# Scan outputs one chunk later, row-half low-rank products, and three moved steps in a hybrid RWKV-7 / attention kernel

## The chip, the cores and the metric

One core of a Trainium2 chip runs the whole step in one launch. The metric is device time in microseconds (us), the median of several runs. The engines named below are PE (TensorE, matrix products), DVE (VectorE), ACT (ScalarE), POOL (GpSimd) and SP (the queue that issues DMAs). Each works through its own list in order.

## The reference, cut to what matters

Two layers work on 1024 latent and 256 context tokens of width 1024. Layer 0 is an RWKV-7 scan in both directions (8 heads of 64) beside a short convolution; layer 1 is grouped-query attention with 16 query and 4 key heads. Each layer is modulated by a vector made from a conditioning input:

```python
mod = silu(cond) @ w_ada + b_ada             # shift, scale, gate
h   = rmsnorm(x, g) * (1 + scale) + shift
# layer 0
w_log = -softplus(-(w0 + tanh(lw) @ lw2)) - 0.5      # low-rank products: 64 wide
decay = exp(-exp(w_log)); a = sigmoid(a0 + la @ la2)
# per head and token, forwards and backwards:
S = S * w_t - (S @ kk_t) (kk_t * a_t)^T + v_t k_t^T ;  y_t = S @ r_t
# layer 1: softmax(q k^T / 8 ...) v, gated, projected
```

## The kernel before, in words

All numbers are fp32. Where a big product is made, its operands are split into a high and a low part, and three matrix products take the place of one (`h_hi,whi`, `h_lo,whi`, `h_hi,wlo`). Every instruction is recorded through one helper, so nearly every row of the trace bears its line, L145; rows are told apart by the names of the tiles.

The order of the work is set while the program is built, by a planner (`Loom`). Each piece of work is a generator that says before each group of instructions what it needs (`yield "T", tiles, rings`: T is PE, V DVE, S ACT, G POOL, D a DMA); among the generators that are ready, the planner takes the first in a list of names (`PRECEDENCE`). The last ones in the list, the big products, fill the gaps. PSUM banks lie in small rings: `mm` (2 banks, the big products), `wk` (2), `py` (2), `iv` (1) and `ch` (1).

The stages, with their times in the trace:

- **0 to 64 us, setup.** Four tiles of x are loaded, then rows of small parameters (`prow`; among them `c` and `c_ctx`), transposed on PE, then eight tiles `wada` of the modulation's weights with three buffers (`ada`). 32 matmuls with `cond` give `mrow`, from which come `mod` and the first normalised inputs `h_hi`, `h_lo`.
- **64 to 1162 us, in-projection and scan.** 2448 big products `mm<-h_hi,whi` and so on run beside 20 scan steps. A step has two heads, two directions and four chunks of 64 tokens. `prepare` makes the low-rank products `iv<-lor,lw` and the decays; `interact` makes products of the keys of a chunk (`wk<-s,bk`) and transposes keys (`tbk`); `solve` inverts the 32 x 32 blocks by 62 DVE instructions on `acc`, which go through DRAM (`w_d`) to the tile `w`; `merge` joins the blocks of `w` to 64 x 64 ones, by `iv<-ident,w` (a transposition on PE), `iv<-t,nn` and `iv<-w,zz`; `chain` runs the four chunks.
- **1162 to 1575 us.** Out-projection of layer 0, then the products of layer 1: gate g0, keys and values, queries, gate g1 (`mm<-h_hi,wts`).
- **1575 to 2130 us, attention.** Maxima of the scores are taken first: pairs of products `kh,qh` (64 rows each), and a DVE reduction `mx` for each. After that come scores `qh,kh`, exponentials, and `pv<-pe,v_sb`.
- **2130 to 2252 us.** The last projection.

A chunk of `chain` has this sequence, each step in four small matmuls: `ch<-hv,s` (the state's part, `pa`); a copy of it to `xs`; `py<-s,hv` (the output's first part); `ch<-xs,w` (`pu`, with the inverse); copies of it to `hv`; `ch<-hv,tbk` (the next state's sum); four DVE instructions `hv<-ch,gc,hg` that make the next state; `py<-br,hv` (the output's second part); and taking both `py` banks out to `y`. The next chunk's `ch<-hv,s` needs the four new `hv`.

What starts a solve and an attention stage is held by two conditions:

```python
yield lambda: x.nr is not None and (x.n < 2 or steps[x.n - 2].done)   # all_solved
yield lambda: 1 not in wk_ps.busy.values()                            # all_moved, "attention"
```

Of the kernel before, what the change touches and what calls it, by code (L numbers as in the profile page):

```python
# [48 lines left out]
              ("evac", -0.1), ("h1", 1.0), ("x", -0.1), ("interacted", 0), ("solved1", 0), ("solved", 0),  # L49
# [67 lines left out]
class Loom:  # L117
# [128 lines left out]
    def issued(self, e, name, a, k, r):  # L246
# [9 lines left out]
        if e == "T":  # L256
# [3 lines left out]
            else:  # L260
                dur = max(0.054, n * (1 if ins[0].dtype == F32R else 4) / 2400.0)
                if ins[0].dtype == F32R and ins[0].partition_size() == 64:
# [66 lines left out]

    def run(self, gens):  # L330

        self.live = [[g, lambda: True, x] for g, x in gens]
# [35 lines left out]
def hybrid_step(  # L368
# [42 lines left out]
        ("c", c.rearrange("o (n p) -> (o n) p", p=P), 8),  # L411
        ("c_ctx", c_ctx.rearrange("(n p) -> n p", p=P), 8),
# [12 lines left out]
    with tc.tile_pool(name="prm", bufs=2, reuse_waits="tile") as prm:  # L425
        r0 = 0
        t0 = 0
# [39 lines left out]

    def ada(pool, cond, jobs):
# [72 lines left out]
    with tc.tile_pool(name="eyep", bufs=1, reuse_waits="tile") as eyep:  # L541
# [353 lines left out]
    def prepare(x):  # L895
# [11 lines left out]
        for d in range(2):  # L907
            yield "T", x.lor, lw2, iv_ps
            pz = iv_ps.take()
            for z in range(2):  # L910
                T.matmul(pz[:, z * GRP:(z + 1) * GRP], lw2[HH[d], z, :], x.lor[HH[d], z, :], start=True, stop=True)
            for z in range(2):
# [3 lines left out]
            iv_ps.release(pz)  # L916
# [64 lines left out]
    def interact(x):  # L981
# [40 lines left out]
        yield lambda: x.n < 2 or steps[x.n - 2].done  # L1022

        x.tbk = chn.tile([P, 2, 4, P], F32, tag="tbk", name="tbk")
# [16 lines left out]
    def solve(x):  # L1041
# [14 lines left out]
        x.solved = True  # L1056
        wdt = wd[x.n % 4]
        dma(out=wdt.rearrange("i p t -> p i t"), in_=acc)
        x.w = w_t[x.n % 2]
        w8 = x.w.rearrange(CD)  # L1060
        for hb_ in range(4):
            b = hb_ % 2
            dma(out=w8[hb_ * 32:hb_ * 32 + 32, :, b * 32:b * 32 + 32],
                in_=wdt.rearrange("i (q c r) t -> r (i q) c t", q=4, r=4)[hb_])

    def merge(x):
# [20 lines left out]
        yield "T", w8, iv_ps  # L1087
        pa = iv_ps.take()
# [6 lines left out]
        yield from copied(pa, *((t11[r:r + 32, :], pa[r:r + 32, 0:256]) for r in (0, 64)))  # L1095
        iv_ps.release(pa)
# [24 lines left out]
    def chain(x):  # L1121
# [33 lines left out]
        yield "T", x.hv[:, :, :, 0], x.s[0], x.s[1], x.w, ch_ps  # L1155
        pc = ch_ps.take()
        for i in range(4):
# [3 lines left out]
            for d in range(2):  # L1161
                for h, rr in enumerate(HH):
                    T.matmul(pa[rr, d], x.s[h][:, d, i, 0, :], x.hv[:, h, d, i, :], start=True, stop=True)
            xs = chn.tile([P, 2, C], F32, tag="xs", name="xs", bufs=1)
            yield from copied(pa, (xs, pa))
            yield "T", py_ps, py_ps
            pys = [py_ps.take(), py_ps.take()]
            for d in range(2):
                for h, rr in enumerate(HH):
                    T.matmul(pys[d][rr, 0:C], x.hv[:, h, d, i, :], x.s[h][:, d, i, 1, :], start=True, stop=False)  # L1170
# [29 lines left out]
            yield ("T",)  # L1200
            for d in range(2):
                for h, rr in enumerate(HH):
                    T.matmul(pys[d][rr, 0:C], x.hv[rr, h, d, i, :], x.br[rr, d, i, :], start=False, stop=True)
            for d in range(2):
                py = pys[d]
                yield "V" if j is not None and j >= 2 else "S", py, 0.15
                c0 = i * C if d == 0 else GRP - (i + 1) * C
                ysl = y[d][:, c0:c0 + C]
                if d == 1:
                    ysl = ysl[:, ::-1]  # L1210
                if (j is not None and j >= 2) or c0 in seen:
                    V.tensor_tensor(out=ysl, in0=py[:, 0:C], in1=ysl, op=ALU.add)
                else:
                    S.activation(ysl, py[:, 0:C], AF.Copy)
                if j is None:
                    seen.add(c0)
                py_ps.release(py)
            if i < 3:
                yield "T", x.hv[:, :, :, i + 1]
# [63 lines left out]
    V.memset(cond, 0.0)  # L1283
    S.activation(cond[:, :, 0], col("c", 0, 8), AF.Silu)
    S.activation(cond[:, :, 1], col("c_ctx", 0, 8), AF.Silu)
# [60 lines left out]
    with tc.high_priority():  # L1346
        for i in range(4):
            get_x(i)
# [1103 lines left out]
```

## Time and profile before

| what | us |
|---|---|
| median of 3 runs (lowest, highest) | 2257.18 (2255.88, 2263.26) |
| the profiled execution's own time | 2253.86 |
| its span, first to last instruction | 2252.2 |
| PE busy in it | 2052.1 (91%) |
| DVE busy | 1471.9 (65%) |
| ACT busy | 1052.1 (47%) |
| POOL busy | 1012.0 (45%) |
| mean granted clock of TensorE | 0.951 |

The span is what the trace covers; the execution's own time is 1.7 us longer. PE is the engine that is busy longest; whether it also sets the end in a stage is read from that stage's rows. A busy PE includes matrix products that wait in its pipeline, so intervals from one start to the next are better prices than durations.

### The profile page before, as it was taken

The numbers are of one execution on the slowest core, as the hardware profiler recorded it, in microseconds if no ns is written. First come the engines' busy times: TensorE is split into PE (matmuls) and PEld (weight loads), VectorE is DVE, ScalarE is ACT, GpSimd is POOL, SyncE is SP. The second block draws the span as 40 slices with busy tenths as digits, with TensorE's granted clock in tenths as the row PEclk, the third lists the DMA queues.
The fourth block names the chain that finished last, engine by engine and source line by source line (L and its number), as shares of the span: only waits on it lengthen the run. The fifth ranks groups of instructions, "written<-read, shape, count | busy, mean of one in ns | idle before, by whom it ended". The sixth has DMA issues, their size and how long they took to land.

```text
span 2252.2 us, 42921 instructions
## 1 busy us (share of the span) xinstructions
PE 2052.1 (91%) x15306; PEld 1411.7 (63%) x15306; DVE 1471.9 (65%) x3483; ACT 1052.1 (47%) x2476; POOL 1012.0 (45%) x1152
## 2 busy tenths in 40 slices
PE   4998889798988988998979999999999999999898
PEld 1486666576666666666657788888454545454487
DVE  2346878948888886868645733552877777775443
ACT  3446556645665556554435632221354444444422
POOL 2434344333344343333224321430487777888622
PEclk7999899999998999999889999999799999999899
DMA  7834344324433333342345633323321211102243
GB/s 271 305 98 131 98 105 131 85 68 114 102 97 103 99 96 101 85 111 54 86 153 185 206 111 88 99 87 107 82 53 48 60 42 38 43 28 71 58 131 108
DMA packets 337818, 232.86 MB, mean 103 GB/s; under 512 B 163890, under 2 KB 289860, under 8 KB 335556
## 3 DMA queue, kind: packets, MB, share of 16 engines
q1 hardware_dynamic: 337604, 230.12, 35.0%
q8 instruction: 120, 1.97, 0.4%
q14 instruction: 94, 0.77, 0.1%
HBM read 166.95 MB, written 57.75 MB: 100 GB/s over the span
## 4 chain that ended last, share of the span: by engine, by line
PE 39%; DVE 9%; DMA 5%; issue 3%; ACT 1%; POOL 1%; SPq 1%; DVEq 0%; POOLq 0%; ACTq 0%
PE mm L145 21%; PE pv L145 8%; PE wk L145 5%; PE py L145 4%; DVE mx L145 3%; DVE rz L145 1%; DVE zs L145 1%; DMA rz<-rz_d 1%; PE ch L145 1%; DVE tmp L145 1%; SPq L145 1%; DVE acc L145 1%; DMA rz_d<-rc 1%; DMA rc<-rz 0%; DVE hv L145 0%
## 5 line engine op out<-in xcount | busy, mean ns | idle before, releaser
L145 POOL TENSOR_TENSOR zs<-zs,pe 128x512 f32<-128x512 f32 x275 | 366.8, 1370 | 34.1 <-ACT pe L145 32.1
L145 PE MATMUL mm<-h_hi,whi 128*128 128x512 f32 (+1 forms) x816 | 336.5, 412 | 4.3 <-ACT whi L145 4.1
L145 PE MATMUL mm<-h_hi,wlo 128*128 128x512 f32 (+1 forms) x816 | 299.3, 367 | 8.1 <-DVE wlo L145 7.2
L145 PE MATMUL mm<-h_lo,whi 128*128 128x512 f32 (+1 forms) x816 | 298.7, 366 | 0.0
L145 POOL TENSOR_TENSOR wlo<-wraw,whi 128x128 fp32r<-128x128 f32 x228 | 111.4, 494 | 246.0 <-ACT whi L145 205.8
L145 PE MATMUL pv<-pe,v_sb 128*64 128x512 f32 (+1 forms) x832 | 200.4, 604 | 0.0
L145 PEld LDWEIGHTS mm<-h_hi,whi 128*128 128x128 f32 x816 | 159.9, 196 | 49.5 <-issue 12.2
L145 PEld LDWEIGHTS mm<-h_hi,wlo 128*128 128x128 f32 x816 | 160.1, 196 | 37.1 <-DVE wlo L145 10.0
L145 DVE TENSOR_TENSOR acc<-acc,tmp 128x60 f32<-128x60 f32 (+23 forms) x620 | 168.0, 273 | 20.8 <-issue 2.9
L145 PE MATMUL mm<-wts,omh 128*128 128x512 f32 x648 | 166.6, 410 | 7.6 <-ACT wts L145 4.0
L145 PEld LDWEIGHTS mm<-h_lo,whi 128*128 128x128 f32 x816 | 161.0, 197 | 14.4
L145 PE MATMUL mm<-wts,h_hi 128*128 128x512 f32 x480 | 151.1, 396 | 0.0
L145 POOL TENSOR_TENSOR hg<-hv,gc 64x128 f32<-64x128 f32 x152 | 65.1, 428 | 185.0 <-DVE hv L145 173.9
L145 PEld LDWEIGHTS mm<-wts,omh 128*128 128x128 f32 x648 | 122.9, 194 | 38.0 <-ACT wts L145 5.3
L145 ACT ACTIVATE whi<-wraw 128x128 fp32r<-128x128 f32 x272 | 80.2, 305 | 78.2 <-DMA wraw<-in_w_in_e_dram 40.3
L145 DVE TENSOR_REDUCE mx<-mm 128x1 f32<-128x512 f32 (+1 forms) x138 | 89.7, 660 | 36.7 <-PE py L145 12.6
L145 DVE SCALAR_TENSOR_TENSOR hv<-ch,gc,hg 64x64 f32<-64x64 f32 x288 | 81.3, 282 | 49.3 <-PE ch L145 42.2
L145 POOL TENSOR_TENSOR xr<-xr,og 128x512 f32<-128x512 f32 x40 | 54.6, 1364 | 128.4 <-DVE og L145 93.3
L145 PEld LDWEIGHTS pv<-pe,v_sb 128*64 128x64 f32 x832 | 51.6, 139 | 93.9 <-issue 82.3
L145 DVE TENSOR_REDUCE mx<-py 128x1 f32<-128x512 f32 (+1 forms) x138 | 89.6, 660 | 28.7 <-PE mm L145 13.0
L145 DVE TENSOR_TENSOR tmp<-acc,nra 128x31 f32<-128x31 f32 (+7 forms) x320 | 90.1, 282 | 27.4 <-DMA acc<-eye_d 17.7
L145 ACT ACTIVATE pe<-py 128x512 f32<-128x512 f32 (+1 forms) x139 | 79.1, 587 | 60.3 <-PE mm L145 20.3
(284 smaller groups left out, 5189.5 us busy)
## 6 DMA issues: line engine op xcount, KB each, us to landing
wraw<-in_w_in_e_dram SPq DMA_DIRECT2D x272, 64.0 KB
wada<-in_w_ada_dram SPq DMA_DIRECT2D x16, 1024.0 KB
inp<-rkv_d SPq DMA_DIRECT2D x40, 384.0 KB
om<-om_d SPq DMA_DIRECT2D x52, 256.0 KB
wraw<-in_w_in_o_dram SPq DMA_DIRECT2D x40, 256.0 KB
wada<-in_w_ada_dram SPq DMA_DIRECT2D x16, 512.0 KB
rkv_d<-nb SPq DMA_DIRECT2D x24, 256.0 KB
lor<-lora_d SPq DMA_DIRECT2D x40, 128.0 KB
```

What stands on the lines that cost most here:

```text
L145: r = f(*a, **k)
```

## The change

1. **Setup.** `c` and `c_ctx` get a tile of their own (`crow`), loaded first and transposed early, so that `cond` is there early. `wada` has five buffers, and five of its loads stand between the loads of x, ahead of the parameter rows.
2. **Low-rank products.** Both directions' banks are taken together (one of the ring `iv`, one of `wk`), and the four matmuls alternate between rows 0 to 63 and rows 64 to 127.
3. **`merge`.** The transposition of `w` on PE (16 matmuls and two copies a step) is made by two DVE transpositions.
4. **Conditions.** The transposition of keys (`tbk`) is a generator of its own. A solve no longer waits for the step two before it to be done; that wait stands now after the result's way to DRAM. Of two solves the older goes first.
5. **`chain`.** One `py` bank for a chunk. `py<-s,hv` stands right behind `ch<-hv,s`; `py<-br,hv` of a chunk right behind the next chunk's `ch<-xs,w`; `y` is taken out a chunk later.
6. **First maxima.** Those of the first three blocks use the two `py` banks, and attention's move of banks waits for them.
7. **Planner.** The cost that the planner books for 64-row matmuls now holds for fp32 too and only for over 64 columns; this changes the order alone.

```diff
@@ ada
-            wt = pool.tile([P, n * 512], F32, tag=f"wada{n}", name="wada")
+            wt = pool.tile([P, n * 512], F32, tag=f"wada{n}", name="wada", bufs=ADA if n == 4 else 3)
...
-        for _ in range(3):
-            get()
+        with tc.high_priority() if not loom.on else nullcontext():
+            for _ in range(3 if loom.on else ADA):
+                get()
+                if not loom.on and len(xts) < 4:
+                    get_x(len(xts))
@@ prepare
-        for d in range(2):
-            yield "T", x.lor, lw2, iv_ps
-            pz = iv_ps.take()
-            for z in range(2):
+        yield "T", x.lor, lw2, iv_ps, wk_ps
+        pzs = [iv_ps.take(), wk_ps.take()]
+        for z in range(2):
+            for d, pz in enumerate(pzs):
                 T.matmul(pz[:, z * GRP:(z + 1) * GRP], lw2[HH[d], z, :], x.lor[HH[d], z, :], start=True, stop=True)
@@ solve
-        x.solved = True
         wdt = wd[x.n % 4]
         dma(out=wdt.rearrange("i p t -> p i t"), in_=acc)
+        yield lambda: x.n < 2 or steps[x.n - 2].done
@@ merge
-        for i in range(8):
-            for h in range(2):
-                r1 = 64 * h
-                T.matmul(pa[r1:r1 + 32, i * 32:i * 32 + 32], w8[r1:r1 + 32, i, 0:32], ident[r1:r1 + 32, r1:r1 + 32],
-                         start=True, stop=True)
...
+        for rr in HH:
+            V.transpose(t11[rr].rearrange("p (i t) -> p i t", i=8), w8[rr, :, 0:32])
@@ chain
+        def by_u(i, py):
+
+            for d in range(2):
+                for h, rr in enumerate(HH):
+                    T.matmul(py[rr, d * C:d * C + C], x.hv[rr, h, d, i, :], x.br[rr, d, i, :], start=False,
+                             stop=(d == 1), skip_group_check=True)
...
+            if before:
+                by_u(i - 1, before)
             yield from copied(pu, *((x.hv[rr, h, :, i, :], pu[rr]) for h, rr in enumerate(HH)))
...
+            if before:
+                yield from put(i - 1, before)
+            before = py
@@ all_solved
-            yield lambda: x.nr is not None and (x.n < 2 or steps[x.n - 2].done)
+            yield lambda: x.ready
+            loom.yield_to(*("solved", "solved1") if b == 0 else ("solved1", "solved"))
@@ all_moved, all_first
-        yield lambda: 1 not in wk_ps.busy.values()
+        yield lambda: 1 not in wk_ps.busy.values() and "first" in moved
...
-            yield from maxima_of(k, 0, 1)
+            yield from maxima_of(k, 0, 1, py_ps)
+        yield lambda: not py_ps.busy
+        moved.add("first")
```

How the instructions stand now. The names are tiles as in the text above; a number behind a name tells one use of a bank or tile from another.

On PE, in the scan, one direction's low-rank products of a step (the other direction's stand some thirty rows away), before:

```order
L145 MATMUL mm_6939<-h_hi,whi 128x512
L145 MATMUL mm_6939<-h_lo,whi 128x512
L145 MATMUL mm_6939<-h_hi,wlo 128x512
L145 MATMUL iv_7202<-lor,lw_6969 128x256 x2
L145 MATMUL ch_6895<-hv,tbk 64x64 x4
```

and both directions' of a step, after:

```order
L145 MATMUL mm_7205<-h_hi,whi 128x512
L145 MATMUL mm_7205<-h_lo,whi 128x512
L145 MATMUL mm_7205<-h_hi,wlo 128x512
L145 MATMUL iv_7222<-lor,lw_7037 128x256
L145 MATMUL wk_7223<-lor,lw_7037 128x256
L145 MATMUL iv_7222<-lor,lw_7037 128x256
L145 MATMUL wk_7223<-lor,lw_7037 128x256
L145 MATMUL ch_6899<-hv,tbk 64x64 x4
```

The four matmuls of a step stand together, and neighbours write to different banks from different row halves.

On PE, in a chunk of the chain in the middle of the scan, from the next state's sum `ch<-hv,tbk` to the next chunk's `ch<-hv,s`, before:

```order
L145 MATMUL ch_12159<-hv,tbk 64x64 x4
L145 MATMUL iv_12318<-ident,vt 64x128 x4
L145 MATMUL py_12258<-br,hv 64x64 x2
L145 MATMUL py_12259<-br,hv 64x64 x2
L145 MATMUL mm_12269<-h_hi,whi 128x512
L145 MATMUL mm_12269<-h_lo,whi 128x512
L145 MATMUL mm_12269<-h_hi,wlo 128x512
L145 MATMUL ch_12159<-hv,s_10532 64x64
L145 MATMUL ch_12159<-hv,s_10533 64x64
L145 MATMUL ch_12159<-hv,s_10532 64x64
L145 MATMUL ch_12159<-hv,s_10533 64x64
```

and after, in a chunk from the product with the inverse on:

```order
L145 MATMUL ch_12255<-xs,w_198 64x64 x4
L145 MATMUL py_12260<-br,hv 64x64 x4
L145 MATMUL mm_12251<-h_hi,whi 128x512
L145 MATMUL mm_12251<-h_lo,whi 128x512
L145 MATMUL mm_12251<-h_hi,wlo 128x512
L145 MATMUL mm_12251<-h_hi,whi 128x512
L145 MATMUL mm_12251<-h_lo,whi 128x512
L145 MATMUL mm_12251<-h_hi,wlo 128x512
L145 MATMUL ch_12255<-hv,tbk 64x64 x4
L145 MATMUL mm_12251<-h_hi,whi 128x512
L145 MATMUL mm_12251<-h_lo,whi 128x512
L145 MATMUL mm_12251<-h_hi,wlo 128x512
```

`py<-br,hv` (now that of the chunk before) has left the stretch behind `ch<-hv,tbk` and stands beside `ch<-xs,w`; big products alone fill the stretch in which the DVE makes the next state.

On PE, at the end of gate g1's products, before, where no product `kh,qh` stands ahead of the last `mm<-h_hi,wts`:

```order
L145 MATMUL mm_17904<-h_hi,wts_17181 128x256
L145 MATMUL mm_17904<-h_hi,wts_17193 128x256
L145 MATMUL mm_17904<-h_lo,wts_17193 128x256
L145 MATMUL mm_17904<-h_hi,wts_17194 128x256
L145 MATMUL mm_17946<-kh_16675,qh_17576 128x512
L145 MATMUL mm_17948<-kh_16675,qh_17576 128x512
L145 MATMUL pv_17964<-kh_16675,qh_17576 128x512
L145 MATMUL py_17966<-kh_16675,qh_17576 128x512
```

and after:

```order
L145 MATMUL mm_17641<-h_lo,wts_16777 128x256
L145 MATMUL mm_17641<-h_hi,wts_16778 128x256
L145 MATMUL py_17689<-kh_16259,qh_17192 128x512
L145 MATMUL py_17691<-kh_16259,qh_17192 128x512
L145 MATMUL py_17696<-kh_16259,qh_17192 128x512
L145 MATMUL py_17698<-kh_16259,qh_17192 128x512
L145 MATMUL wk_17723<-ident,qt_17172 128x128 x4
L145 MATMUL pv_17731<-qh_17160,kh_16259 128x512
```

24 of the 26 pairs of the first maxima now stand among gate g1's products, about nine 512-column products apart; two pairs are left behind the last one, and the first scores `qh,kh` follow.

## Rows read from the trace of the kernel before

**Rows 1.** Busy time by stretch: us, PE, PEld, DVE, ACT, POOL, PEclk, DMA share, GB/s

```profile
14.00:20.00 6.00, 0.91 (x8) 0.25 (x12) 4.46 (x20) 1.11 (x3) 0.85 (x4) 1.00 1.00 418
100.00:1100.00 1000.00, 899.45 (x9092) 666.50 (x9092) 753.93 (x2155) 549.73 (x1439) 388.10 (x645) 0.95 0.37 100
1100.00:1160.00 60.00, 45.98 (x412) 28.40 (x410) 36.09 (x105) 23.21 (x57) 12.06 (x17) 0.77 0.44 136
1575.00:1585.00 10.00, 9.01 (x25) 4.12 (x25) 10.00 (x18) 1.63 (x3) 3.28 (x4) 0.84 0.97 275
1575.00:1604.50 29.50, 27.01 (x56) 12.79 (x56) 29.50 (x58) 4.15 (x7) 5.77 (x6) 0.62 0.60 154
```

**Rows 2.** Waits of PE, 100 to 1170 us: us in total, times, longest

```profile
PE ch L145 <- DVE hv L145: 19.7, 30, 2.8
PE ch L145 <- ACT hv L145: 7.0, 19, 1.5
```

**Rows 3.** Setup by time: start, us, engine, operation, [idle before <-releaser]

```profile
12.12 20.00 SPq L145 DMA_DIRECT2D wada<-in_w_ada_dram  x8
...
39.79 1.93 PE L145 MATMUL wk<-wada,cond 128*32 128x512 f32 x8 [2.61 <-DMA wada<-in_w_ada_dram]
41.79 0.69 DVE L145 COPY mrow<-wk 128x512 f32<-128x512 f32 x1 [23.10 <-PE wk L145]
```

**Rows 4.** PE groups of 0 to 1170 us: xcount, busy us, mean ns, idle before

```profile
L145 PE MATMUL iv<-lor,lw 64*128 64x256 f32 x160 | 48.8, 428 | 3.3 <-ACT bk L145 1.1 <-DMA lor<-lora_d 1.1 <-DVE y L145 0.7
L145 PE MATMUL iv<-ident,w 32*32 32x32 f32 x640 | 14.7, 195 | 4.5 <-DMA w<-w_d 1.9 <-DVE y L145 1.6 <-ACT sqy L145 0.6
```

**Rows 5.** PE by time in mid-scan

```profile
540.90 0.40 PE L145 MATMUL mm<-h_lo,whi 128*128 128x512 f32 x1
541.14 0.40 PE L145 MATMUL mm<-h_hi,wlo 128*128 128x512 f32 x1
...
558.81 1.13 PE L145 MATMUL iv<-lor,lw 64*128 64x256 f32 x4
559.87 0.45 PE L145 MATMUL ch<-hv,tbk 128*64 128x64 f32 x8
560.25 0.45 PE L145 MATMUL wk<-s,bk 64*64 64x128 f32 x8
560.52 0.34 PE L145 MATMUL py<-br,hv 64*64 64x64 f32 x6
...
562.14 0.45 PE L145 MATMUL wk<-s,bk 64*64 64x128 f32 x8
562.52 0.45 PE L145 MATMUL py<-s,hv 128*64 128x64 f32 x8
```

**Rows 6.** DVE groups of 0 to 1170 us

```profile
L145 DVE SCALAR_TENSOR_TENSOR hv<-ch,gc,hg 64x64 f32<-64x64 f32 x288 | 81.3, 282 | 49.3 <-PE ch L145 42.2 <-ACT bk L145 2.3 <-ACT nb L145 0.9
...
L145 DVE COPY hv<-iv 64x256 f32<-64x256 f32 x10 | 4.2, 418 | 0.2
```

**Rows 7.** PE by time, from gate g1's last product to attention

```profile
1573.98 0.28 PE L145 MATMUL mm<-h_hi,wts 128*128 128x256 f32 x1
...
1609.57 0.50 PE L145 MATMUL wk<-kh,qh 64*128 64x512 f32 x1
1609.91 0.39 PE L145 MATMUL mm<-qh,kh 64*128 64x512 f32 x1
...
1612.11 1.94 PE L145 MATMUL pv<-pe,v_sb 128*64 128x512 f32 x8
```

**Rows 8.** DVE by time, the same stretch

```profile
1563.73 0.69 DVE L145 SCALAR_TENSOR_TENSOR sgo<-sgo,mm 128x512 f32<-128x512 f32 x1 [4.91 <-ACT sgo L145]
...
1575.05 1.36 DVE L145 TENSOR_REDUCE mx<-mm 128x1 f32<-128x512 f32 x2
...
1590.51 0.20 DVE L145 STREAM_TRANSPOSE mt<-mx 128x32 f32<-128x32 f32 x1
```

**Rows 9.** The queue SP by time, the same stretch

```profile
1577.74 0.51 SPq L145 DMA_DIRECT2D v_sb<-v_d  x1
```

More of the change, by code (lines that the diff above doesn't have):

```diff
@@ L425, in hybrid_step @@
     with tc.tile_pool(name="prm", bufs=2, reuse_waits="tile") as prm:
+        with tc.high_priority():
+            crow = prm.tile([16, P], F32, name="crow", bufs=1)
+            for i, x in enumerate((c.rearrange("o (n p) -> (o n) p", p=P), c_ctx.rearrange("(n p) -> n p", p=P))):
+                dma(out=crow[8 * i:8 * i + 8, :], in_=x)
+            pt = py_ps()
+            T.transpose(out=pt[:, 0:16], in_=crow, identity=ident[0:16, 0:16])
+            V.tensor_copy(par[:, 0:16], pt[:, 0:16])
+        rows["c"], rows["c_ctx"] = 0, 8
         r0 = 0
-        t0 = 0
+        t0 = 16
         cur = prm.tile([P, P], F32, tag="prow", name="prow")
@@ L1153, in chain, with put @@
                 ch_ps.release(pt)
-        yield "T", x.hv[:, :, :, 0], x.s[0], x.s[1], x.w, ch_ps
+        def by_u(i, py):
[3 more added lines that the diff above has]
+                             stop=(d == 1), skip_group_check=True)
+        def put(i, py):
+            for d in range(2):
+                c0 = i * C if d == 0 else GRP - (i + 1) * C
+                ysl = y[d][:, c0:c0 + C]
+                if d == 1:
+                    ysl = ysl[:, ::-1]
+                add = (j is not None and j >= 2) or c0 in seen
+                yield "V" if add else "S", py, 0.3
+                if add:
+                    V.tensor_tensor(out=ysl, in0=py[:, d * C:d * C + C], in1=ysl, op=ALU.add)
+                else:
+                    S.activation(ysl, py[:, d * C:d * C + C], AF.Copy)
+                if j is None:
+                    seen.add(c0)
+            py_ps.release(py)
+        yield "T", x.hv[:, :, :, 0], x.s[0], x.s[1], x.w, ch_ps, py_ps
         pc = ch_ps.take()
+        before = None
         for i in range(4):
@@ L1163, in chain @@
                     T.matmul(pa[rr, d], x.s[h][:, d, i, 0, :], x.hv[:, h, d, i, :], start=True, stop=True)
+            py = py_ps.take()
+            for d in range(2):
+                for h, rr in enumerate(HH):
+                    T.matmul(py[rr, d * C:d * C + C], x.hv[:, h, d, i, :], x.s[h][:, d, i, 1, :], start=(d == 0),
+                             stop=False, skip_group_check=True)
             xs = chn.tile([P, 2, C], F32, tag="xs", name="xs", bufs=1)
             yield from copied(pa, (xs, pa))
[L1166 to L1170, printed above, removed]
             if not last:
@@ L1199, in chain @@
                                                in1=hg[rr, d], op0=ALU.mult, op1=ALU.add)
[L1200 to L1217, printed above, removed]
+            if before:
+                yield from put(i - 1, before)
+            before = py
             if i < 3:
-                yield "T", x.hv[:, :, :, i + 1]
+                yield "T", x.hv[:, :, :, i + 1], py_ps
+        yield ("T",)
+        by_u(3, before)
+        yield from put(3, before)
         ch_ps.release(pc)
@@ L1344, in all_h @@
             h_made[b] += 1
-    with tc.high_priority():
-        for i in range(4):
-            get_x(i)
+    first = ada(adap, cond, [(0, 0, 4)])
+    next(first)
     for _ in norm_x(0, 4):
         pass
-    for _ in ada(adap, cond, [(0, 0, 4)]):
+    for _ in first:
         pass
@@ L2060, in hybrid_step, with maxima_of @@
     maxima = []
-    def maxima_of(k, part, parts):
+    def maxima_of(k, part, parts, banks=mm_ps):
         f, b = PAIRS[k]
@@ L2137, in all_maxed @@
             if maxima:
-                pt, w, out, left = maxima[0]
+                pt, w, out, left, banks = maxima[0]
                 yield "V", pt
                 V.tensor_reduce(out=out, in_=pt[:, 0:w], axis=AX.X, op=ALU.max)
-                mm_ps.release(pt)
+                banks.release(pt)
                 maxima.pop(0)
```

50 lines of the change are left out of this document (29 added, 21 removed).

## Prediction

> **What bounds the kernel now.** I read the busy time by stretch first. From 100 to 1100 us, where the in-projection and the scan run together, PE is busy 899 of 1000 us, DVE 754, ACT 550, DMA at 0.37 [rows 1]. So PE's own work is what a change there has to lower, unless the remaining 100 us of idle grow. The waits of PE say what those are: the longest entry is `ch` on DVE's `hv`, 19.7 us in 30 waits, the next state of the chain; `ch` on ACT's `hv`, the copy after the inverse, has 7.0 us in 19 waits [rows 2]. There are 76 chunks with such a place, so PE waits at 30 of 76. Other stretches have other limits: up to 41.8 us PE and DVE wait for the modulation's weights [rows 3]; from 1575 to 1604.5 DVE is busy 29.50 of 29.50 us, PE runs at a granted clock of 0.62, and PE's work there is only the first maxima [rows 1].
>
> **Setup.** All eight `wada` loads (1 MB each) are issued at 12.12 us; the last one's matmuls start at 39.79 and end at 41.7, and `mrow` follows at 41.79 after 23.1 us of idle DVE [rows 3]. After the change five of them and the four tiles of x are issued from about 2 us: 7.3 MB at the 418 GB/s of 14 to 20 us [rows 1] are 17.5 us, so they are there at about 20. The parameter rows queue behind them on SP, and PE's transposition of those rows stands ahead of the first `wada` matmul: I put PE's start at 24. The sixth load needs a buffer that PE has read, so the last three megabytes go from about 25 to 35, and the last matmul ends at about 37 in place of 41.7. I take -4.5 us. Bounds: 0 (the queue's order costs what the buffers give) and -10 (all loads shifted by the 10 us between 2 and 12).
>
> **Low-rank products.** 160 records of `iv<-lor,lw` are busy 48.8 us [rows 4]; a group of four (two instructions) takes 1.06 us from 558.81 to 559.87 [rows 5], and a step has two groups. If neighbours on rows 0 to 63 and 64 to 127 run together, a step's 2.12 us become 1.06: 20 x 1.06 = 21 us less. For running together speak two rows. Four `wk<-s,bk` instructions of 128 columns (eight records) take 0.27 us [rows 5], where half of a low-rank instruction's 0.53 us each would make 1.06. And a pair of 64-row `kh,qh` of 512 columns, which start at the same time, takes 0.34 us from 1609.57 to 1609.91 [rows 7], while a single 128-row product of 512 columns takes 0.24 [rows 5]. Those pairs go to two banks, as the changed low-rank products do. Bounds 0 and -21; I take -21.
>
> **The transposition in `merge`.** 640 records of `iv<-ident,w` are busy 14.7 us, 0.735 us in each of 20 groups [rows 4]; a group's successor starts some 0.07 us before its end [rows 5], so 13 us of PE leave. DVE gets 40 transpositions of 64x256. That shape is not in the trace: a 128x32 one takes 0.20 us [rows 8], a copy of 64x256 0.418 [rows 6]. I take 0.42, the nearer in size: 17 us. The planner also gives DVE 22 more copies of the turned keys, by the same row 9 us. These 26 us lie in the 246 us that DVE has free between 100 and 1100 [rows 1]; without that cover they would cost 26.
>
> **Order on PE.** A group of eight `wk<-s,bk` records takes 0.27 us where the next group has the same form (64*64) and 0.38 where the next has another (128*64) [rows 5]: a change of form costs 0.11 us. Up to the scan's last chain PE's order has 798 changes of form before and 615 after, since `py<-s,hv` now stands behind `ch<-hv,s` and `py<-br,hv` behind `ch<-xs,w`, each of its neighbour's form. 183 x 0.11 = 20 us less. Bounds 0 (the changes hide in waits) and -20; I take -20.
>
> The Trainium skill, "TensorEngine Tiling (Array Packing)", Key Properties, says that changing the tiling mode drains the engine. The 0.27 against 0.38 us agrees with it; without such a drain this term would be nothing and the sum below 20 us smaller, and the 24 pairs of maxima that are now put among full-size products would be cheaper by 3 us.
>
> **What the chain loses.** Between `ch<-hv,tbk` and the next `ch<-hv,s` PE must fill the time of four `hv` instructions of 0.282 us [rows 6], 1.13 us and the way there and back. `py<-br,hv` has left this stretch. With 0.24 us for a product, 0.38 for a group of the chain [rows 5], the median of PE work there goes from 1.71 to 1.40 us by the order, 0.31 less; in front of `ch<-hv,tbk` it rises from 1.21 to 1.45. If all of some 70 places felt the first, it would cost 21 us; I take the 30 of 76 that wait now, 8 us. The second could return up to the 7.0 us of waits there; I leave it as a bound. The solves that start earlier queue more DVE instructions ahead of `hv`; their cover is again DVE's free time. After the change the last two steps' chains stand behind the last in-projection product, one before; that stretch has PE at 46 of 60 us and a clock of 0.77 [rows 1]. I book nothing for it, since what PE lacks there it did earlier.
>
> Scan: -21 - 13 - 20 + 8 = -46 us. Its bounds: +34 (13 us of gain alone, against 21 of new waits and 26 of DVE), and -81 (54 of PE work, 19.7 and 7.0 of waits).
>
> **First maxima.** The last g1 product ends at 1574.2 [rows 7], the reductions start at 1575.05 [rows 8], and the first `pv` starts at 1612.11 [rows 7]: 37.9 us. During g1 DVE sits idle 4.9 us between two `sgo` [rows 8], so 24 pairs' reductions, 1.3 us a pair, fit between products nine of which take 2.1 us: the two `py` banks are free again in time. A pair costs PE 0.34 and one change of form more on the way back, 0.45; 24 are 10.8 us. What is late next is `v_sb`: its last part, 1.3 MB, is issued at 1577.74 [rows 9], 3.5 us after g1's end, and at 275 GB/s beside other loads [rows 1] needs 4.8 us and its landing. I put the first `pv` at 10.5 us behind g1. Gain: 37.9 - 10.5 - 10.8 = 16.6 us. Bounds -10 (pairs stall for their banks) and -27 (pairs at 0.24, `v_sb` early).
>
> **Sum.** -4.5 - 46 - 16.6 = -67 us against the profiled execution's 2253.86 gives 2187; the median of the runs lies 3.3 us above that execution, so 2190.
>
> **Rivals.**
> - *The scan gives its gain back.* PE's groups shrink, but the chain of state, copy, inverse and next state keeps its length; PE then idles for what it no longer does. For it: the waits on `hv` are already the longest [rows 2]. Against: PE at 0.90 with filler products at hand in nearly all of the scan. The scan is then worth 0, the rest -21: 2236.
> - *The scan also loses its waits.* More distance in front of `ch<-hv,tbk`, earlier solves and one `py` bank a chunk take away the 27 us of chain waits: -81 - 21 = -102, so 2155. Against: the cover of the longer of the two waits becomes shorter.
> - *Row halves stay one after the other*, or another instruction between them spoils it: 21 us less gain, 2211.
> - *Slower: the chain stands behind DVE.* DVE works in order; solves without the old condition, transpositions and key copies stand ahead of a chunk's four `hv`. The gain of 67 us is gone at 0.88 us per chunk (76 chunks), two instructions of 0.42 us; with three, 1.26 x 76 = 96 us, the time is 2286. For it: DVE is the second busiest engine, 0.75. Against: 26 us of new work on 20 steps is 1.3 us a step, not a chunk.
>
> **How the numbers follow.** Forecast 0.42, waits lost too 0.17, row halves apart 0.13, scan gives back 0.22, slower 0.06. The likeliest one's own range is 2172 to 2208. The range for 8 in 10 reaches into the second and takes in most of the first rival: 2158 to 2238. A measurement of this kernel tells 0.3%, 6.8 us, from no change: faster has the first three cases and most of the fourth, 0.91; same 0.04; slower 0.05.
>
> **What would show it.** Low-rank groups of 1.06 us in place of two, with starts in pairs; no `iv<-ident,w`; `ch<-hv,s` with `py<-s,hv` behind it in 0.27 to 0.28 us; PE's waits for `hv` at 20 to 35 us; the last in-projection product some 45 us earlier, PE filled by the out-projection some 50 us earlier; the first `wada` matmul at about 24 us and `mod` 4 us earlier; `mx` reductions among the `sgo`, and 10 us from g1's end to `pv`. I am wrong if the in-projection's PE share falls to 0.85 (the scan gave back), or if the waits for DVE's `hv` pass 80 us.

## The result and the profile after

The changed kernel takes 2277.35 us (median of 6 runs, 2270.22 to 2283.40) against 2256.53 for the kernel before (6 runs, 2247.12 to 2263.26): ratio 1.0094, interval 1.0070 to 1.0119. It is 21 us slower; 2190 was forecast. The profiled execution of after has a span of 2281.7 us and a granted clock of 0.938 (before 2252.2 and 0.951), so its stages tell of 29.5 us, 9 more than the medians.

Where they went, by stage: setup to `mrow` -0.8; from there to gate g1's last product +46; from g1 to the first `pv` -29.6 (38.1 to 8.5); from the first `pv` to the end +13.9. Up to the last joined inverse of the scan (1138.6 before, 1160.0 after) 22 of the 46 us are there; 15 of the rest are the pairs of first maxima that now stand inside g1.

Busy time by stretch, after (columns as in [rows 1]):

```profile
100.00:1100.00 1000.00, 855.59 (x8159) 638.07 (x8158) 762.43 (x2112) 518.12 (x1349) 380.70 (x626) 0.91 0.37 98
1100.00:1160.00 60.00, 47.61 (x522) 33.15 (x520) 49.16 (x176) 25.50 (x59) 10.70 (x17) 0.89 0.42 113
```

PE is busy 856 us in place of 899 [rows 1], which is near the 0.85 that was to mean "the scan gave back", and its granted clock fell from 0.95 to 0.91. (The trace's records of the clock hold two levels, full and half (2.4 and 1.2 GHz); such a figure is the mean over a stretch.)

Waits of PE, 100 to 1200 us, after:

```profile
PE ch L145 <- DVE hv L145: 47.8, 39, 3.6
PE iv L145 <- DVE t L145: 21.7, 14, 4.8
```

The first was 19.7 us in 30 waits [rows 2]. The second is new: `t` is what the DVE transposition writes. The single operations of the scan do what was forecast. PE by time, after, both directions of a step's low-rank products:

```profile
168.60 0.48 PE L145 MATMUL iv<-lor,lw 64*128 64x256 f32 x1
168.60 0.48 PE L145 MATMUL wk<-lor,lw 64*128 64x256 f32 x1
...
169.35 0.38 PE L145 MATMUL iv<-lor,lw 64*128 64x256 f32 x1
169.36 0.38 PE L145 MATMUL wk<-lor,lw 64*128 64x256 f32 x1
169.66 0.50 PE L145 MATMUL mm<-h_hi,whi 128*128 128x512 f32 x1
...
545.20 0.45 PE L145 MATMUL ch<-hv,s 128*64 128x64 f32 x8 [1.19 <-DVE hv L145]
545.48 0.40 PE L145 MATMUL py<-s,hv 128*64 128x64 f32 x8
```

They start in pairs and take 1.06 us a step, where one direction alone took 1.06 [rows 5]. `py<-s,hv` follows `ch<-hv,s`, of its own form, in 0.28 us. DVE's group of the new transposition, 0 to 1200 us, after (count, busy us, mean ns):

```profile
L145 DVE STREAM_TRANSPOSE t<-w 64x256 f32<-64x256 f32 x40 | 17.4, 436 | 2.4 <-DMA w<-w_d 1.7
```

Forecast was 0.42 us each, 17 us in all.

Setup by time, after:

```profile
25.23 7.94 PE L145 MATMUL wk<-wada,cond 128*32 128x512 f32 x48 [0.28 <-DVE par L145]
...
36.47 1.51 PE L145 MATMUL wk<-wada,cond 128*32 128x512 f32 x8 [3.29 <-DMA wada<-in_w_ada_dram]
...
39.00 1.94 PE L145 MATMUL wk<-wada,cond 128*32 128x512 f32 x8 [1.02 <-DMA wada<-in_w_ada_dram]
41.00 0.69 DVE L145 COPY mrow<-wk 128x512 f32<-128x512 f32 x1 [12.93 <-PE wk L145]
```

PE starts the first product at 25, as forecast (24), but the last load lands at 39.0, not 35, and `mrow` comes 0.8 us earlier than in [rows 3].

First maxima, PE by time, after:

```profile
1574.77 0.50 PE L145 MATMUL py<-kh,qh 64*128 64x512 f32 x2
1575.21 0.50 PE L145 MATMUL mm<-h_hi,wts 128*128 128x512 f32 x1
...
1577.50 0.50 PE L145 MATMUL py<-kh,qh 64*128 64x512 f32 x2
...
1619.28 0.28 PE L145 MATMUL mm<-h_hi,wts 128*128 128x256 f32 x1
...
1627.78 1.94 PE L145 MATMUL pv<-pe,v_sb 128*64 128x512 f32 x8
```

and DVE, same stretch:

```profile
1616.81 0.41 DVE L145 SCALAR_TENSOR_TENSOR sgo<-sgo,mm 128x256 f32<-128x256 f32 x1
...
1617.99 1.29 DVE L145 TENSOR_REDUCE mx<-py 128x1 f32<-128x512 f32 x2 [0.17 <-PE py L145]
```

The reductions lie among the `sgo`, and the first `pv` comes 8.5 us behind g1 (10.5 forecast, 38.1 in [rows 7]). A pair with nine products takes 2.73 us, nine products alone 2.1: 0.63 for a pair, not 0.45, so 24 pairs cost 15 us, not 10.8. The forecast's 0.34 was that of the first pair behind another form; pairs of 64 rows in a row start 0.23 us apart. PE by time, before:

```profile
1609.91 0.39 PE L145 MATMUL mm<-qh,kh 64*128 64x512 f32 x1
...
1610.14 0.39 PE L145 MATMUL mm<-qh,kl 64*128 64x512 f32 x1
```

### The profile page after: what moved, and what is told of

It is laid out like the page before. It is cut to its first block, busy times and chain, and to the rows that moved or that the text cites. A ratio compares the mean times of both kernels' runs of the same rounds, so it can differ in the third digit from the quotient of the medians.

```text
span 2281.7 us, 41720 instructions
## 1 busy us (share of the span) xinstructions
PE 2026.6 (89%) x14667; PEld 1397.7 (61%) x14667; DVE 1520.0 (67%) x3546; ACT 1035.1 (45%) x2422; POOL 1019.5 (45%) x1151
## 4 chain that ended last, share of the span: by engine, by line
PE 39%; DVE 13%; DMA 7%; issue 4%; SPq 2%; ACT 2%; POOL 1%; DVEq 0%; POOLq 0%; ACTq 0%
PE mm L145 20%; PE pv L145 7%; PE py L145 5%; PE wk L145 5%; DVE mx L145 2%; DVE tmp L145 2%; DVE acc L145 2%; SPq L145 2%; DVE rz L145 1%; DVE hv L145 1%; DMA rz<-rz_d 1%; DVE zs L145 1%; PE ch L145 1%; DMA rz_d<-rc 1%; PE iv L145 1%
## 5 line engine op out<-in xcount | busy, mean ns | idle before, releaser
L145 PE MATMUL pv<-pe,v_sb 128*64 128x512 f32 (+1 forms) x832 | 205.1, 616 | 0.0
L145 DVE TENSOR_TENSOR acc<-acc,tmp 128x60 f32<-128x60 f32 (+24 forms) x620 | 172.2, 278 | 19.4 <-issue 1.3
L145 PE MATMUL mm<-wts,omh 128*128 128x512 f32 x624 | 162.0, 412 | 8.8 <-ACT wts L145 4.1
L145 DVE TENSOR_REDUCE mx<-py 128x1 f32<-128x512 f32 (+1 forms) x173 | 111.1, 661 | 55.3 <-PE py L145 27.9
L145 DVE TENSOR_TENSOR tmp<-acc,nra 128x31 f32<-128x31 f32 (+7 forms) x320 | 102.7, 321 | 34.8 <-DMA acc<-eye_d 25.1
L145 PE MATMUL mm<-h_hi,wts 128*128 128x512 f32 (+1 forms) x384 | 111.1, 364 | 0.0
L145 ACT ACTIVATE pe<-mm 128x512 f32<-128x512 f32 (+1 forms) x140 | 80.8, 588 | 55.1 <-PE mm L145 20.8
```

The source lines that it names most:

```text
L145: r = f(*a, **k)
```

## The experiments

Each median stands beside that of the kernel before in the same session, with the ratio and its 95% interval. Where only one median is given, it stands beside the one named last for the kernel before. The changed kernel (2277.35) was timed in the first session alone; the kernel before came to between 2256.2 and 2259.4 in all of them, so a distance from the changed kernel is good to some 3 us beyond the spread of the runs. Unless a text says otherwise a diff is against the kernel before; `...` marks what is left out of it.

### One part alone, one part undone

**only_halves**: part 2 alone.

```diff
-            yield "T", x.lor, lw2, iv_ps
+        yield "T", x.lor, lw2, iv_ps, wk_ps
...
```

> The kernel before with one edit: both directions' low-rank products taken together in two banks, row halves alternating. Theory A (PE's work sets the scan; halves run together): a group of four low-rank instructions takes 1.06 us, 21 us of PE leave, 2232 to 2242 us against 2256. Theory B (the scan's length is set by its chain of steps and by DVE, and PE only fills): low-rank groups of 1.06 us all the same, PE idle grows by as much, 2250 to 2262 us. Theory C (halves do not run together): 2.1 us per step remain, 2256.

2277.97 against 2259.01, 1.0078 [1.0050, 1.0105]. The halves run together, PE has 23 us less to do, and the kernel is 19 us slower: outside all three theories.

**no_dve_transpose**: the changed kernel without part 3.

```diff
-            V.transpose(t11[rr].rearrange("p (i t) -> p i t", i=8), w8[rr, :, 0:32])
...
+                T.matmul(pa[r1:r1 + 32, i * 32:i * 32 + 32], w8[r1:r1 + 32, i, 0:32], ...
```

> The changed kernel with the transposition in merge back on PE (16 matmuls and two copies a step). Theory A (PE's work sets the scan): 13 us more, about 2290. Theory D1 (the DVE transpositions, queued in DVE's order, hold up merge and with it the chain: PE waited 21.7 us for t on DVE): those waits go, and with them 10 to 25 us, 2250 to 2267.

2273.35, 1.0062 [1.0036, 1.0089]: 4 us better than the changed kernel, within the spread of either. Neither theory's range holds it.

**old_conditions**: the changed kernel without part 4.

```diff
-            yield lambda: x.ready
+            yield lambda: x.nr is not None and (x.n < 2 or steps[x.n - 2].done)
...
```

> The changed kernel with the conditions of before: a solve starts only when the step two before it is done, keys are turned inside interact. Theory D2 (solves that start early put their DVE instructions ahead of the chain's hv: PE's waits for hv went from 19.7 to 47.8 us): waits for hv fall to about 20 us, 2245 to 2260. If D1 or D3 holds, no change within 8 us of 2277.

2289.82, 1.0136 [1.0107, 1.0166]: 12 us worse, and PE's waits for `hv` stay at 46.3 us. Taking the earlier solves back does not give the loss back; neither expectation came out.

**old_chain**: the changed kernel without part 5.

```diff
-            if before:
-                by_u(i - 1, before)
...
```

> The changed kernel with the chain as before: two py banks a chunk, the output's second part behind the next state's sum. Theory D3 (the moved output part took PE's cover for the DVE's hv away, 0.31 us per chunk): waits for hv fall by some 20 us, 20 us of form changes come back, 2270 to 2280. If D2 holds, waits for hv stay above 40 us and the time rises by the form changes, 2285 to 2300.

2258.29, 0.9995 [0.9972, 1.0017]: 19 us of the loss gone, more than either theory had; the waits for `hv` fell to 31.3 us. **only_chain**, part 5 alone, looked at the same from the other side:

```diff
+            if before:
+                by_u(i - 1, before)
...
+            before = py
```

> The kernel before with the chain's part alone: one py bank a chunk, output's second part one chunk later. PE loses form changes, DVE's work stays. Theory B with order: PE's saving is worth nothing, hv's cover and the new order decide: 2255 to 2280. By the prediction's terms for this part (-20 of form changes, +8): 2245.

2294.01 against 2256.34, 1.0163 [1.0139, 1.0186]: 38 us worse, with 24 us less work for PE, and above both ranges. **first_maxima** has part 6 alone:

```diff
+            yield from maxima_of(k, 0, 1, py_ps)
+        yield lambda: not py_ps.busy
+        moved.add("first")
...
```

> The kernel before with the first maxima alone moved into gate g1; nothing ahead of that stage changes. By the prediction's term, 10.8 us for the pairs: 16 us less, 2243. By the trace of the changed kernel, where a pair costs 0.63 us (15 us), the first pv comes 30 us earlier behind g1, and attention then takes 4 to 13 us longer: 2248 to 2260.

2242.20 against 2257.28, 0.9924 [0.9895, 0.9953]: 15 us faster; the term in the forecast was 16.6. If the terms add, the other parts together cost some 36 us. Parts 1 and 7 were not tried by themselves: 7 changes the order alone, and it stands in every kernel here that undoes one part.

### Work taken from PE and DVE, or added, in an unchanged order

**pe_less** (kernel before, 102 products fewer):

```diff
+            if b == 0 and k % 3 == 1:
+                loom.issued("T", "matmul", (pt[:, 0:n], hi, xl), {}, None)   # booked, not issued
...
```

> The kernel before with every engine's order unchanged, and 102 of the 2448 in-projection products left out (the middle one of three, h_lo,whi, for one of three k in the first block of tokens; that part of the product is missing from the output). At 0.233 us each PE has 24 us less to do. Theory A (PE's work sets the scan): 2232 to 2237. Theory B (the chain of steps, DVE on it, sets it, and PE only fills): 2250 to 2258, with PE's idle time 15 to 24 us higher.

2258.89 against 2259.44, 1.0001 [0.9973, 1.0029]: no change, as theory B had it within a us.

**pe_more** (each low-rank product issued twice):

```diff
+                tc.keep_in_program_order(nc.tensor.matmul(
+                    pz[:, z * GRP:(z + 1) * GRP], lw2[HH[d], z, :], x.lor[HH[d], z, :], start=True, stop=True))
```

> The kernel before, same order, every low-rank matmul issued twice: 80 instructions of 0.53 us, 42 us more for PE. Theory A: 2295 to 2300. Theory B: 2262 to 2280, since part of it goes into time in which PE waited.

2283.00, 1.0109 [1.0068, 1.0149]: +24 us, between the two theories. Work left out among the fillers gave nothing; work added to the products that stand ahead of a step's keys is paid for.

**dve_more** (an extra multiplication in every fourth step of a solve):

```diff
+            if t % 4 == 3:
+                tc.keep_in_program_order(nc.vector.tensor_tensor(out=tmp[:, 0:64]..., op=ALU.mult))
```

> The kernel before, same order on PE, ACT and SP; in each of the 20 solves 7 more DVE instructions of 128x64 whose result nothing uses (140 of 0.24 us, 34 us of DVE). Theory A: DVE has a quarter of its time free, 2256 to 2264. Theory B: DVE's work lies on the chain, 2275 to 2292.

2278.53, 1.0100 [1.0067, 1.0134]: +19 us, as theory B had it. **after_dve_less** is the changed kernel with every fourth addition of a solve left out:

```diff
-            V.tensor_tensor(out=acc[:, 0:m, t + 1:32], in0=acc[:, 0:m, t + 1:32], in1=u, op=ALU.add)
+            if t % 4 != 3:
+                V.tensor_tensor(out=acc[:, 0:m, t + 1:32], in0=acc[:, 0:m, t + 1:32], in1=u, op=ALU.add)
```

> The changed kernel, same order on PE, ACT and SP; of the 62 DVE instructions of a solve the 7 additions at t = 3, 7, ... 27 are left out (their terms are missing from the inverse): 140 of 0.28 us, 39 us of DVE. Theory B (DVE, in its order, sets the scan of the changed kernel): by the 0.6 us per us of the run with more DVE work, 20 to 28 us less, 2249 to 2258, and PE's waits for hv fall from 47.8 to under 35 us. If PE or the chain's own length sets it: 2270 to 2278.

2259.99 against 2257.28, 1.0011 [0.9994, 1.0027]: 17 us faster than the changed kernel, 2 us above theory B's range; PE's waits for `hv` fell to 41.9 us only, not under 35.

Busy time by stretch, from 64 us to g1's end, one fence a kernel: before, after,

```profile
64.00:1574.20 1510.20, 1383.16 (x11557) 1039.02 (x11556) 1005.55 (x2664) 743.04 (x1859) 537.80 (x777) 0.96 0.40 113
```

```profile
64.00:1619.50 1555.50, 1377.62 (x10957) 1033.71 (x10957) 1074.02 (x2775) 726.55 (x1803) 543.61 (x775) 0.93 0.39 110
```

pe_less, dve_more and only_halves:

```profile
64.00:1580.30 1516.30, 1373.88 (x11449) 1031.46 (x11447) 1008.68 (x2662) 741.49 (x1858) 539.57 (x776) 0.95 0.39 113
```

```profile
64.00:1593.80 1529.80, 1386.04 (x11539) 1041.97 (x11538) 1033.99 (x2800) 741.11 (x1855) 536.21 (x774) 0.95 0.39 112
```

```profile
64.00:1587.00 1523.00, 1367.34 (x11548) 1033.64 (x11540) 1005.49 (x2670) 734.48 (x1840) 537.08 (x777) 0.95 0.39 112
```

Each stretch is the sum of three: PE's work at full clock (busy time times granted clock, summed over the trace's records), busy time lost to the lower clock, and idle:

| us | before | after | pe_less | pe_more | dve_more | only_halves | no_halves | prepared_early |
|---|---|---|---|---|---|---|---|---|
| work | 1327 | 1289 | 1299 | 1359 | 1322 | 1304 | 1307 | 1287 |
| lost to the clock | 56 | 88 | 74 | 58 | 64 | 63 | 83 | 71 |
| idle | 127 | 178 | 142 | 119 | 144 | 156 | 190 | 170 |

Each column is one profiled execution. Executions of one order differ too: first_maxima has the order of before up to 1528 us, and its last joined inverse comes at 1130.1 us, not 1138.6. In pe_less 28 us of work less (24 by the price of 102 products) came back as 18 us of lower clock and 15 of idle; that execution was 7 us longer than the one of before, where the medians agree. Where PE idled more than before, the clock term is larger too: a gap seems to cost twice. In dve_more DVE's busy time rose by 28 us and the stretch by 20, although DVE is busy only two thirds of it: solves seem to stand in what sets the pace.

### The same program in another order

**other_order** changes only the planner's bias for DVE, **after_other_order** the same in the changed kernel, **dearer_dve** the changed kernel's price for DVE, **order_and_maxima** is other_order with part 6.

```diff
-BIAS = {"V": 0.3, "sum": 3.0}
+BIAS = {"V": 0.33, "sum": 3.0}     # other_order, after_other_order
-COST = {"V": (0.065, 1.04e-3), ...
+COST = {"V": (0.12, 1.04e-3), ...  # dearer_dve, the bias unchanged
```

> The kernel before with one number of the planner changed (its preference against DVE, 0.30 to 0.33 us), which alters no work, only the order of some 2600 PE rows and which of DVE and ACT makes some copies. Theory O (the order that the planner comes to moves the scan by as much as the parts do): differs from 2256 by more than 8 us, either way. If the order matters little: within 6 us.

2245.08 against 2259.44, 0.9937 [0.9916, 0.9957]: 14 us faster, no work changed.

> The changed kernel with the planner's preference against DVE at 0.33 us, no work changed. Theory O (the planner's order is worth as much as a part): differs from 2277 by over 8 us; it was -14 on the kernel before. Otherwise 2270 to 2284.

2253.43 against 2256.34, 0.9991 [0.9971, 1.0011]: 24 us faster than the changed kernel.

> The changed kernel with DVE's price in the planner raised by 0.055 us an instruction, nearer to the trace; work is the same, only order and the choice between DVE and ACT change. Theory B with order: DVE gets fewer copies and the chain's hv stand less far behind other DVE work: 2245 to 2265. If the planner's order does not matter: 2277.

2271.70 against 2257.28, 1.0072 [1.0045, 1.0099]: 6 us faster than the changed kernel, between the two expectations and not clear of the spread.

> The kernel before with the planner's preference against DVE at 0.33 us and the first maxima moved: the two edits that looked best. If they add: 2245 less 0 to 12 us, 2233 to 2245.

2240.00, 0.9920 [0.9894, 0.9946], within the expected 2233 to 2245. It beats both kernels, as first_maxima (2242.20) does; the 14 and the 15 us do not add: on this order the first maxima are worth 5 us (2240.00 against 2245.08).

### Is the wait for `hv` the cause?

In the changed kernel `hv` waits longer behind instructions of a solve. DVE by time, after, and PE under it:

```profile
569.24 0.22 DVE L145 TENSOR_TENSOR acc<-acc,tmp 128x60 f32<-128x60 f32 x1
569.49 0.24 DVE L145 TENSOR_TENSOR tmp<-acc,nra 128x76 f32<-128x76 f32 x1
569.64 1.17 DVE L145 SCALAR_TENSOR_TENSOR hv<-ch,gc,hg 64x64 f32<-64x64 f32 x4
```

```profile
567.36 0.45 PE L145 MATMUL ch<-hv,tbk 128*64 128x64 f32 x8
...
570.87 0.45 PE L145 MATMUL ch<-hv,s 128*64 128x64 f32 x8 [1.47 <-DVE hv L145]
```

From the end of `ch<-hv,tbk` to the first `hv` 71 us pass over 76 chunks, 39 before: 0.42 us a chunk more. For 36 of the 71 us DVE is busy with solves, for 18 of the 39 before. **after_hv_early** and **best_hv_early** (on order_and_maxima) let up to four solve instructions pass behind `hv` in DVE's list, at 26 of 76 places in the changed kernel:

```diff
+                            while len(loom.held) > HOLD:     # HOLD = 4
+                                loom.let_go(1)
...
+                        if name != "scalar_tensor_tensor" or not loom.first:
+                            loom.let_go()
```

> The changed kernel, same order on PE, ACT and SP; on DVE the four hv instructions of a chunk go up to four solve instructions earlier in its list where solve instructions stand right ahead of them (26 of 76 places); no work is added or left out. Theory E (the chain is late because hv stands behind solve instructions in DVE's list): the time from ch<-hv,tbk to hv falls from 71 us in sum to about 50, the whole by 10 to 25 us, 2252 to 2267. If DVE's total work alone counts, and not its order: 2272 to 2280.

2294.64 against 2256.34, 1.0169 [1.0140, 1.0198]: 17 us worse than the changed kernel, where theory E had 10 to 25 us less. But the edit hardly did what it was for: the 71 us went to 69, not to about 50. PE's waits for `hv`, 100 to 1200 us, after_hv_early, then order_and_maxima and best_hv_early:

```profile
PE ch L157 <- DVE hv L157: 42.7, 37, 3.5
```

```profile
PE ch L145 <- DVE hv L145: 19.1, 32, 1.4
```

```profile
PE ch L157 <- DVE hv L157: 13.9, 28, 1.3
```

> The same move of hv in the kernel before with the planner's number 0.33 and the first maxima moved (2240 us). There hv waits behind solve instructions for 14 of 42 us. Theory E: 2230 to 2238. If only DVE's total counts: 2240.

2247.95, 0.9965 [0.9945, 0.9984]: 8 us worse than order_and_maxima, again against theory E. Each time a wait that got 5 us shorter came with a longer time. What the wait costs is not settled by this, since most of it stayed in the changed kernel; but this way of shortening it does not pay.

### The loop of two steps

Work goes round in a loop: the joined inverse of step n-2 lets the key products of step n start (`wk<-s,bk`), their result goes through DRAM (`n_d`), a solve follows, its result goes through DRAM (`w_d`) and is joined (`iv<-w,zz`). Means over steps 2 to 17, in us (the start of a solve is the issue of its load `acc<-eye_d`):

| stretch | before | after | prepared_early | no_halves |
|---|---|---|---|---|
| inverse of n-2 to first key product of n | 5.9 | 16.4 | 6.9 | 14.6 |
| key products to `n_d` | 14.8 | 15.4 | 15.7 | 14.1 |
| `n_d` to the start of the solve | 11.1 | 5.5 | 5.7 | 5.6 |
| solve to `w_d` | 44.7 | 40.8 | 44.5 | 41.4 |
| `w_d` to the joined inverse | 17.8 | 18.7 | 19.7 | 22.4 |
| two steps | 94.3 | 96.8 | 92.5 | 98.1 |

The means hide a wide spread: two steps take 73 to 120 us before. Part 4 did its work: the solve starts 5.6 us earlier behind `n_d` (its first DVE instruction 4.6). The first stretch lost 10.5. PE by time, after, one of the long cases: low-rank products of step 8, joined inverse of step 6, low-rank products of step 9, first key product of step 8:

```profile
530.67 0.48 PE L145 MATMUL iv<-lor,lw 64*128 64x256 f32 x1
...
548.92 0.69 PE L145 MATMUL iv<-w,zz 32*32 32x32 f32 x32 [0.57 <-issue]
...
579.69 0.48 PE L145 MATMUL iv<-lor,lw 64*128 64x256 f32 x1
...
585.78 0.45 PE L145 MATMUL wk<-s,bk 64*64 64x128 f32 x8
```

POOL, after, the last part of step 8's keys:

```profile
566.27 0.73 POOL L145 TENSOR_TENSOR bk<-inp,cum 128x256 f32<-128x256 f32 x1
```

and a short case of the kernel before, PE:

```profile
821.84 0.69 PE L145 MATMUL iv<-w,zz 32*32 32x32 f32 x32 [1.49 <-ACT zz L145]
823.36 0.45 PE L145 MATMUL wk<-s,bk 64*64 64x128 f32 x8
```

The last keys come 17 us behind the inverse, and the products another 19 behind the keys, with the next step's low-rank products, which hold a `wk` bank, in between. On average the 16.4 us are 5.0 until the keys of the first direction, which the first product reads, are there, and 11.4 from then on (before: 0.5 and 5.4). So keys that are not there yet are the smaller part of it.

**prepared_early** is the changed kernel with one name moved in the planner's list:

```diff
-              ... ("interacted", 0), ("tbk", 0), ("solved1", 0), ("solved", 0), ("finished", 0.1), ("prepared", 0), ...
+              ... ("interacted", 0), ("prepared", 0), ("tbk", 0), ("solved1", 0), ("solved", 0), ("finished", 0.1), ...
```

> The changed kernel with one entry of the planner's list of names moved: the generator that prepares a step (low-rank products, decays, keys) stands right behind the one that makes the products of the keys, ahead of transposition and solves; every part of the change stays. Theory (prepare comes too late): between the end of one step's joined inverse and the first key products of the step two on, the changed kernel spends 16.4 us on average and the kernel before 5.9, because the prepared keys are not there yet. In PE's new order the number of big products in that stretch falls from 35 to 14 (before: 16), so the wait falls to 8 us or less, two steps take 90 to 93 us in place of 98, and the median is 2245 to 2262. Rival (any new order shifts the time at random by up to 24 us, whatever this wait does): a median anywhere from 2253 to 2300, and the two-step time not below 95.

2253.90 against 2256.24, 0.9986 [0.9967, 1.0004]: 23 us faster than the changed kernel, as the theory had it. The wait falls to 6.9 us and two steps to 92.5 (96.8 in the changed kernel by the same means). The median alone lies in the rival's range too (2253 to 2300); what speaks against the rival is the two steps. The edit also moves much else: DVE's list after it keeps hardly half of its old sequence. The last joined inverse, PE by time, in before, after and prepared_early:

```profile
1137.52 1.06 PE L145 MATMUL iv<-w,zz 32*32 32x32 f32 x32 [2.52 <-issue]
```

```profile
1159.27 0.69 PE L145 MATMUL iv<-w,zz 32*32 32x32 f32 x32 [0.52 <-DVE y L145]
```

```profile
1122.65 1.07 PE L145 MATMUL iv<-w,zz 32*32 32x32 f32 x32 [0.52 <-DVE y L145]
```

**no_halves** is the changed kernel without part 2:

```diff
-        yield "T", x.lor, lw2, iv_ps, wk_ps
+            yield "T", x.lor, lw2, iv_ps
...
```

> The changed kernel with part 2 undone: each direction's low-rank products take the bank iv alone, one after the other. Theory (prepare comes too late): in PE's order the stretch between inverse and the next key products stays at 31 big products (35 in the changed kernel), so the wait stays at 13 us or more and PE has 21 us more work that mostly fills idle time: median 2268 to 2285. Rival (the two banks taken at once are what holds prepare up): the wait falls to 8 us or less, the median to 2262 or less.

2308.42, 1.0251 [1.0212, 1.0289]: 31 us worse than the changed kernel, a miss: 2268 to 2285 was expected. The wait stayed long (14.6 us), as the theory had it, so the second bank is not what holds it up; but 18 us more work for PE cost 31. The same edit that cost 19 us alone is worth 31 here.

The loop is not the only end of this stretch. In only_chain and no_dve_transpose the last inverse comes earlier than before, and both kernels are slower: there the in-projection's own last product is 45 and 40 us late. That product before, then last inverse and last such product in only_chain and in no_dve_transpose:

```profile
1110.66 0.40 PE L145 MATMUL mm<-h_hi,wlo 128*128 128x512 f32 x1
```

```profile
1132.79 0.69 PE L145 MATMUL iv<-w,zz 32*32 32x32 f32 x32
...
1155.25 0.40 PE L145 MATMUL mm<-h_hi,wlo 128*128 128x512 f32 x1
```

```profile
1118.86 0.69 PE L145 MATMUL iv<-w,zz 32*32 32x32 f32 x32
...
1150.78 0.39 PE L145 MATMUL mm<-h_hi,wlo 128*128 128x512 f32 x1
```

## Why the prediction was wrong

- **The step that failed** is the first one: "PE's own work is what a change there has to lower, unless the remaining 100 us of idle grow", and with it the scan's sum of -46. The term itself was right in size: PE's work from 64 us to g1's end fell by 38 us, and without the 15 us of pairs that are inside it by 53, where 21, 13 and 20 had been counted. But idle grew by 51 us, and the loss to the clock, for which the sum has no term, by 32. That less work for PE does not by itself shorten the scan is shown: taking work out in an unchanged order moved nothing (pe_less). The share of 0.90 was read as "PE sets the pace"; much of it was in-projection products filled in around the loop of two steps. The Trainium skill, "Perfetto Trace Analysis", Identifying the Most-Contended Engine, says that the busy share of matmuls is not a good measure of how close a kernel is to the roofline, and judges PE's headroom by other figures. Those figures are not tested here; pe_less shows that at a busy share of 0.90 there was no gain in less work.
- **What took its place**: the key products of a step come 10.5 us later behind the inverse, two steps take 96.8 us, not 94.3, and the last inverse comes 21 us later (pe_less and first_maxima, in the order of before, have it 8 us later and 8 us earlier). prepared_early fits this: with the stretch back at 6.9 us the changed kernel is as fast as before. It does not prove that the stretch alone makes the loss, since it moves much else and after_other_order gains as much with the stretch at 14. prepared_early too gains nothing over the kernel before from 40 us less work, the 15 us of pairs already counted in: its idle is 170 us.
- **Order on PE**: a change of form was priced at 0.11 us and 183 went. In the order that came with them, part 5 alone cost 38 us. The term "what the chain loses", +8, met +28 us of waits for `hv` (47.8 against 19.7); what these waits cost stays open, since the two runs that were to shorten them took off 5 us each and were slower.
- **DVE's 26 us** were booked at nothing because DVE had 246 us free. Free time is no cover for work in a solve: dve_more's 28 us cost 19. Undoing the transposition gave only 4 us back, not clearly.
- **Setup**: -0.8, not -4.5; the last loads still waited for their place and landed at 39.
- **First maxima**: -16.6 forecast, -15 alone, -5 on other_order. That -15 lies so near is in part luck: in first_maxima's profile 8.5 us are gained up to the last inverse, where no instruction is changed; behind it, the way to g1's end is 13 us longer, `pv` comes 28 us nearer, and attention to the end takes 10 us more, for which nothing was booked. In the changed kernel's profile the nearer `pv` gives 29.6 us, the pairs take 15, and attention to the end is 13.9 us longer, with PE at a granted clock of 0.96 in place of 0.97 between the first and the last `pv`, and 4 us more of waits for `mx`.
- **The rivals**: "the scan gives its gain back" named the right mechanism, idle in place of work, and priced it at zero; it went on below zero. The slower rival had the right side, but not its size: the waits for `hv` came to 47.8 us, under the 80 that were to show it, and whether they decide is open. That the planner's order alone can move the time by 14 to 24 us (other_order, after_other_order) had no chance of its own.

**Still open**: what makes the changed kernel 21 us slower is argued, not shown. It is not known why the planner's new order brings preparation and key products later, nor what part 7, which every kernel with one part undone keeps, does to it. Undoing any one of parts 2 to 5 leaves the stretch at 11 to 15 us, and parts 2 and 5 alone give about 10. The stretch is not the only thing in an order that counts either: old_chain and after_other_order have 14 us there and still take 2253 to 2258.

## What to carry over

Before work is counted as gain, ask what the loop is: follow one step round to the same point of the step that depends on it, and see whether the change shortens a stretch of that circle; an engine at 0.90 can be filled rather than full. A cheap test is to leave a little of its work out in an unchanged order. Where a planner sets the order, a change of 15 us can't be judged from one order: here one constant moved the time by 14 to 24 us, so each part should be tried in several, and its time should choose among them: here neither the longest wait in the list nor the longest stretch of the loop told by itself which order is fast.

## What the hardware showed that was not expected

- With work left out of PE its granted clock was lower: 0.944 in the mean over pe_less's 10 runs, 0.950 over the 20 of the kernel before beside them. From 64 us to g1's end of the profiled executions the loss to the lower level rose from 56 to 74 us with 28 us of work less (pe_less), to 88 in the changed kernel.
- A pair of 64-row products between full ones cost 0.63 us, where such pairs in a row follow each other in 0.23 (before, from 1609.91 us).
- Two low-rank products on rows 0 to 63 and 64 to 127, into two banks, start within 0.01 us of each other and take the time of one.
